# The first load of six rows goes over two DMA queues instead of one

## The chip, the cores and the metric

The kernel runs on one core of one Trainium2 chip. Its time is the device time in microseconds of one execution, and the figure for a kernel is the median of its runs. Beside the timed runs, one execution was taken by the hardware profiler. All durations in the text come from that execution.

## The reference

There are 16 x 1024 = 16,384 tokens with a hidden size of 512, and eight experts. For each token the router's logits are turned into probabilities, the two largest are kept and normalized, and the token's row of x is written out twice, each copy multiplied by one of the two weights:

```
probs        = softmax(router_logits)                    # (16, 1024, 8)
topk_indices = argsort(probs)[..., -2:]
topk_probs   = probs at topk_indices, divided by their sum
out          = x[:, :, None, :].repeat(2, axis=2) * topk_probs[..., None]
```

The output (16, 1024, 2, 512) is twice as large as x. All is float32. The two normalized weights of a token depend only on the difference of its two largest logits.

## The kernel before, in words

**Tiling.** 128 partitions hold 128 tokens of each row index. A token's 512 values are 2 KB, so a "row" of the kernel is 128 tokens, 2 KB on each partition. There are 128 rows in two groups, `GROUPS = [65, 63]`. Within a group each partition holds consecutive tokens, so a load of n rows is, for each of the 128 partitions, one contiguous run of n x 2 KB in HBM.

**Buffers.** `xs` holds the x rows of a group (65 rows of 512 values on each partition). `osp` holds 18 output rows (each 2 x 512). Output rows are written either to `osp` or into parts of `xs` whose input rows have been used up. `WA` holds the two weights of all rows. The logits and the scratch space for finding the two largest lie in `osp`, too, before any output does.

**Order.** The loads of the first group are of 6, 28 and 31 rows, those of the second of 16, 16 and 31 (`LOADS`). Right after the load of six rows come the two loads of the logits, L125 and L126. All of these loads are issued by SyncE (SP), in program order, so they go through one DMA queue in that order. `top2_weights` (L26 to L38) follows: VectorE finds the two largest by maxima and minima, L36 takes the difference into `dlt`, and ScalarE (ACT) makes the two weights with two sigmoids (L37, L38), ahead of which stands the load of its function table.

**The multiplies and stores.** For each piece of `STORES`, VectorE multiplies the x rows by the weights (L133), and a DMA stores the piece (L145). The first piece has three rows, and its store is issued by ACT on its own DMA queue; all other stores are issued by SP. The loads of the second group wait until the stores out of `xs` have freed their places.

SP's queue is called q1 in the profile and ACT's q10. "SPq" and "ACTq" are the instructions on those engines that issue DMAs.

Of the kernel before, what the change touches and what calls it, by code (L numbers as in the profile page):

```python
# [1 line left out]

# [4 lines left out]

F32 = mybir.dt.float32
ALU = mybir.AluOpType
ACTF = mybir.ActivationFunctionType  # L10
P = 128


def top2_weights(nc, WA, dlt, room, logits, E):

    tt = nc.vector.tensor_tensor
    hi, lo, n = None, None, E  # L20
    while n > 1:
        n //= 2
        if hi is None:
            a, b = logits[:, :, 0:n], logits[:, :, n : 2 * n]
            nhi, nlo = room(n), b
            tt(nhi, a, b, op=ALU.max)  # L26
            tt(nlo, a, b, op=ALU.min)  # L27
        else:
            a, b = hi[:, :, 0:n], hi[:, :, n : 2 * n]
            nhi, nlo, tmp = room(n), room(n), room(n)  # L30
            tt(tmp, lo[:, :, 0:n], lo[:, :, n : 2 * n], op=ALU.max)  # L31
            tt(nlo, a, b, op=ALU.min)  # L32
            tt(nlo, nlo, tmp, op=ALU.max)  # L33
            tt(nhi, a, b, op=ALU.max)  # L34
        hi, lo = nhi, nlo
    tt(dlt, hi[:, :, 0], lo[:, :, 0], op=ALU.subtract)  # L36
    nc.scalar.activation(WA[:, :, 0], dlt, ACTF.Sigmoid, scale=-1.0)  # L37
    nc.scalar.activation(WA[:, :, 1], dlt, ACTF.Sigmoid, scale=1.0)  # L38

GROUPS = [65, 63]

LOADS = [[6, 28, 31], [16, 16, 31]]
BASE = [0, 1]

STORES = [
    [(0, 3, "osp", 0), (3, 15, "osp", 3), (18, 16, "xs", 0), (34, 15, "osp", 0), (49, 16, "xs", 33)],
    [(0, 16, "osp", 2), (16, 16, "xs", 0), (32, 15, "osp", 0), (47, 16, "xs", 32)],
]  # L50

L = 18

FREE = [3, 2]


@with_exitstack
def kernel(
    ctx: ExitStack,
    tc: tile.TileContext,  # L60
    x: bass.AP,
    router_logits: bass.AP,
    k: bass.AP,
    out: bass.AP,
):
    nc = tc.nc
    B, S, D = x.shape
    E = router_logits.shape[-1]
    N = B * S
    assert int(k) == 2 and E == 8 and N == P * sum(GROUPS)  # L70
    M = N // P

    x_v, o_v, rl_v = [], [], []
    t0 = 0
    for n in GROUPS:
        t1 = t0 + P * n
        x_v.append(
            x.rearrange("b s d -> (b s) d")[t0:t1].rearrange("(p m) d -> p m d", p=P)
        )
        o_v.append(  # L80
            out.rearrange("b s k d -> (b s) k d")[t0:t1].rearrange(
                "(p m) k d -> p m k d", p=P
            )
        )
        rl_v.append(
            router_logits.rearrange("b s e -> (b s) e")[t0:t1].rearrange(
                "(p m) e -> p m e", p=P
            )
        )
        t0 = t1  # L90

    wpool = ctx.enter_context(tc.tile_pool(name="wpool", bufs=1))
    xs = wpool.tile([P, max(GROUPS), D], F32)
    osp = wpool.tile([P, L, 2, D], F32)
    WA = wpool.tile([P, M, 2], F32)
    dlt = wpool.tile([P, M], F32)


    flat = osp.rearrange("p l k d -> p (l k d)")
    taken = [0]  # L100

    def room(n):
        o = taken[0]
        taken[0] += M * n
        return flat[:, o : o + M * n].rearrange("p (m n) -> p m n", n=n)

    logits = room(E)

    def place(where, at, n):

        if where == "osp":
            return osp[:, at : at + n]
        return xs[:, at : at + 2 * n, :].rearrange("p (r k) d -> p r k d", k=2)

    m0 = 0
    for g, G in enumerate(GROUPS):
        x0, r = BASE[g], 0
        for n in LOADS[g]:
            tc.keep_in_program_order(
                nc.sync.dma_start(xs[:, x0 + r : x0 + r + n, :], x_v[g][:, r : r + n, :])  # L120
            )
            r += n
            if g == 0 and r == 6:
                n0 = GROUPS[0]
                tc.keep_in_program_order(nc.sync.dma_start(logits[:, :n0], rl_v[0]))  # L125
                tc.keep_in_program_order(nc.sync.dma_start(logits[:, n0:], rl_v[1]))  # L126
                top2_weights(nc, WA, dlt, room, logits, E)
        assert r == G
        for r, n, where, at in STORES[g]:
            og = place(where, at, n)  # L130
            again = where == "osp" and at == 0 and r > 0
            for a, b in [(0, FREE[g]), (FREE[g], n)] if again else [(0, n)]:
                nc.vector.tensor_tensor(  # L133
                    og[:, a:b],
                    xs[:, x0 + r + a : x0 + r + b, :]
                    .unsqueeze(2)
                    .to_broadcast([P, b - a, 2, D]),
                    WA[:, m0 + r + a : m0 + r + b, :]
                    .unsqueeze(3)
                    .to_broadcast([P, b - a, 2, D]),  # L140
                    op=ALU.mult,
                )

            queue = nc.scalar if g == r == 0 else nc.sync
            tc.keep_in_program_order(queue.dma_start(o_v[g][:, r : r + n], og))  # L145
        m0 += G


# [1 line left out]
_INS = ['x', 'router_logits', 'k']  # L150
_OUTS = [((16, 1024, 2, 512), 'float32')]

_NUMBERS = {'k': 2}


# [26 lines left out]
```

## Time and profile before

| | |
|---|---|
| median of 3 runs | 240.02 us (239.95 to 240.07) |
| the profiled execution | 239.92 us |
| its span | 238.1 us |
| VectorE busy | 141.9 us (60%) |
| ScalarE busy | 1.8 us |
| read from HBM, written to it | 34.08 MB, 67.11 MB |
| DMA over the span | 425 GB/s on average, 2448 packets |
| queue q1 (SP), q10 (ACT) | 99.62 MB, 1.57 MB |

The span runs from the first to the last recorded instruction of the execution; the profiled execution's own time is 1.8 us longer. The page's DMA row gives the mean busy share of the core's 16 DMA engines in forty slices of the span. A DMA is split into packets, each of which one of the 16 DMA engines carries out. In this kernel a packet is one partition's contiguous run, so a load or store on 128 partitions has 128 packets, and each engine gets eight. A small completion packet per engine follows. The record of a packet has its queue, start, size and duration; it does not name the engine.

A group in a view of busy time by stages counts a packet's bytes and time in the stretch where the packet starts, so a share can be above 1 in a short stretch and below it in the next.

### The profile page before, as it was taken

What the parts mean: (1) busy time and instruction counts of PE and PEld (TensorE: products, weight loads), DVE (VectorE), ACT (ScalarE), POOL (GpSimd) and SP (SyncE); (2) the same over time, 40 slices, a digit from 0 to 9 for tenths busy, and PEclk for the clock granted to TensorE, in tenths of its full rate; (3) what the DMA queues carried; (4) which work ended last, traced back from release to release, by engine and by line L of the source; (5) the groups of instructions that cost most, each with busy time, mean ns of one, the idle gap of its engine ahead of it and who ended that gap; (6) DMA issues with size and microseconds to landing.
All of it is one profiled execution on the core that took longest, in us unless ns stands there. A gap on an engine that the chain in (4) does not pass through costs nothing.

```text
span 238.1 us, 102 instructions
## 1 busy us (share of the span) xinstructions
DVE 141.9 (60%) x22; ACT 1.8 (1%) x3; POOL 0.2 (0%) x4
## 2 busy tenths in 40 slices
DVE  0650499999699999100000699999406999950000
ACT  2000000000000000000000000000000000000000
POOL 0000000000000000000000000000000000000000
DMA  7979998979999999989899999898989999989894
GB/s 265 550 337 500 430 418 374 506 330 495 429 429 407 473 423 402 495 352 528 352 440 435 435 446 501 352 495 374 506 374 462 418 407 451 475 351 517 352 528 176
DMA packets 2448, 101.19 MB, mean 425 GB/s; under 512 B 272, under 2 KB 400, under 8 KB 528
## 3 DMA queue, kind: packets, MB, share of 16 engines
q1 hardware_dynamic: 2304, 99.62, 97.2%
q10 hardware_dynamic: 144, 1.57, 1.5%
HBM read 34.08 MB, written 67.11 MB: 425 GB/s over the span
## 4 chain that ended last, share of the span: by engine, by line
DMA 48%; DVE 40%; SPq 1%; issue 0%; DVEq 0%
DMA xs<-in_x_dram 26%; DVE osp L133 25%; DMA out_dram<-osp 22%; DVE xs L133 14%; SPq L125 0%; SPq L126 0%; SPq L120 0%; SPq L145 0%; DVEq L133 0%
## 5 line engine op out<-in xcount | busy, mean ns | idle before, releaser
L133 DVE TENSOR_TENSOR osp<-xs,WA 128x3072 f32<-128x3072 f32 (+5 forms) x7 | 69.4, 9908 | 61.6 <-DMA xs<-in_x_dram 47.5
L133 DVE TENSOR_TENSOR xs<-xs,WA 128x16384 f32<-128x16384 f32 x4 | 68.9, 17224 | 0.1
L26 DVE TENSOR_TENSOR osp<-osp 128x512 f32<-128x512 f32 x1 | 0.7, 692 | 8.1 <-DMA osp<-in_router_logits_dram 8.1
L37 ACT ACT_TABLE_LOAD x1 | 1.3, 1283 | 0.7 <-PEq L163 0.7
L27 DVE TENSOR_TENSOR osp<-osp 128x512 f32<-128x512 f32 x1 | 0.7, 691 | 0.0
L34 DVE TENSOR_TENSOR osp<-osp 128x256 f32<-128x256 f32 (+1 forms) x2 | 0.7, 352 | 0.0
L32 DVE TENSOR_TENSOR osp<-osp 128x256 f32<-128x256 f32 (+1 forms) x2 | 0.7, 352 | 0.0
L31 DVE TENSOR_TENSOR osp<-osp 128x256 f32<-128x256 f32 (+1 forms) x2 | 0.7, 352 | 0.0
L33 DVE TENSOR_TENSOR osp<-osp 128x256 f32<-128x256 f32 (+1 forms) x2 | 0.7, 351 | 0.0
L37 ACT ACTIVATE WA<-dlt 128x128 f32<-128x128 f32 x1 | 0.3, 314 | 10.1 <-DVE dlt L36 10.1
L36 DVE TENSOR_TENSOR dlt<-osp 128x128 f32<-128x128 f32 x1 | 0.3, 291 | 0.0
L38 ACT ACTIVATE WA<-dlt 128x128 f32<-128x128 f32 x1 | 0.3, 298 | 0.0
L163 POOL MEMSET const-bfloat16-1.0<- 128x1 bf16 x1 | 0.1, 101 | 0.0
L163 POOL MEMSET const-uint8-127<- 128x1 uint8 x1 | 0.1, 101 | 0.0
L163 POOL MEMSET const-float32-0.0<- 128x1 f32 x1 | 0.1, 98 | 0.2 <-issue 0.2
L163 POOL MEMSET const-float32-1.0<- 128x1 f32 x1 | 0.1, 98 | 0.0
## 6 DMA issues: line engine op xcount, KB each, us to landing
out_dram<-osp SPq DMA_DIRECT2D x3, 7680.0 KB, 23.4
xs<-in_x_dram SPq DMA_DIRECT2D x2, 7936.0 KB, 41.7
xs<-in_x_dram SPq DMA_DIRECT2D x2, 4096.0 KB, 40.4
xs<-in_x_dram SPq DMA_DIRECT2D x1, 7168.0 KB, 24.8
xs<-in_x_dram SPq DMA_DIRECT2D x1, 1536.0 KB, 6.0
out_dram<-osp ACTq DMA_DIRECT2D x1, 1536.0 KB, 24.8
osp<-in_router_logits_dram SPq DMA_DIRECT2D x1, 260.0 KB, 6.2
osp<-in_router_logits_dram SPq DMA_DIRECT2D x1, 252.0 KB, 6.4
```

The lines of the kernel that those rows point to most:

```text
L26: tt(nhi, a, b, op=ALU.max)
L27: tt(nlo, a, b, op=ALU.min)
L31: tt(tmp, lo[:, :, 0:n], lo[:, :, n : 2 * n], op=ALU.max)
L32: tt(nlo, a, b, op=ALU.min)
L33: tt(nlo, nlo, tmp, op=ALU.max)
L34: tt(nhi, a, b, op=ALU.max)
L36: tt(dlt, hi[:, :, 0], lo[:, :, 0], op=ALU.subtract)
L37: nc.scalar.activation(WA[:, :, 0], dlt, ACTF.Sigmoid, scale=-1.0)
L38: nc.scalar.activation(WA[:, :, 1], dlt, ACTF.Sigmoid, scale=1.0)
L133: nc.vector.tensor_tensor(og[:, a:b], xs[:, x0 + r + a : x0 + r + b, :] .unsqueeze(2) .to_broadcast([P, b - a, 2, D]), WA[:, m0 + r + a : ...
L163: nc = _bacc.Bacc("TRN2", target_bir_lowering=False, num_devices=1)
```

## The change

The first load of the first group, six rows, is split by partitions. SP loads partitions 0 to 63 and ACT loads partitions 64 to 127 of the same six rows. All other loads stay as they were, on SP with all 128 partitions.

```diff
         for n in LOADS[g]:
-            tc.keep_in_program_order(
-                nc.sync.dma_start(xs[:, x0 + r : x0 + r + n, :], x_v[g][:, r : r + n, :])
-            )
+
+            halves = [(nc.sync, 0, P // 2), (nc.scalar, P // 2, P)]
+            for queue, p0, p1 in halves if g == r == 0 else [(nc.sync, 0, P)]:
+                tc.keep_in_program_order(
+                    queue.dma_start(
+                        xs[p0:p1, x0 + r : x0 + r + n, :], x_v[g][p0:p1, r : r + n, :]
+                    )
+                )
             r += n
```

On SP the first instruction that issues a DMA now covers 64 partitions x 3,072 values instead of 128 x 3,072; the number and order of its instructions stay. On ACT one new DMA (64 x 3,072) stands first, ahead of the load of the function table, the two sigmoids and the store. VectorE's list of instructions is the same.

## The prediction

> **What bounds the kernel now.** I read the page's busy table and its slices first, then busy time by stages, then the timeline and the waits of the start, then the records of single DMA packets.
>
> ```profile
> DVE 141.9 (60%) x22; ACT 1.8 (1%) x3; POOL 0.2 (0%) x4
> DMA  7979998979999999989899999898989999989894
> DMA packets 2448, 101.19 MB, mean 425 GB/s; under 512 B 272, under 2 KB 400, under 8 KB 528
> ```
>
> No compute engine is busy all the time: VectorE has 60%. The DMA row is full in nearly every slice. Busy time by stages (columns: stretch, length, DVE, ACT, POOL, clock, DMA share, GB/s) says the same with less noise:
>
> ```profile
> 0.00:1.70 1.70, 0.00 (x0) 0.98 (x1) 0.20 (x4) 1.00 0.00 0
> 1.70:6.40 4.70, 0.00 (x0) 0.30 (x1) 0.00 (x0) 1.00 0.98 364
> 6.40:20.00 13.60, 7.18 (x12) 0.51 (x2) 0.00 (x0) 1.00 1.02 433
> 45.00:236.90 191.90, 116.68 (x9) 0.00 (x0) 0.00 (x0) 1.00 0.99 429
> 236.90:238.10 1.20, 0.00 (x0) 0.00 (x0) 0.00 (x0) 1.00 0.00 0
> ```
>
> From 1.7 us to 236.9 us the sixteen DMA engines work without a pause. The first load (1.70 to 6.40) is the one stage below the usual rate, 364 against 429 to 433 GB/s. The packet records show why: each engine takes eight packets of 12,288 B, one per partition, in sixteen-wide waves. The first wave starts at 1.73 to 2.35 us and its packets take 949 ns on average; those of the seven waves after it take 460 to 495 ns on average. So the opening latency costs about 0.5 us, once. Later packets are paced almost exactly: 2,116 ns for 57,344 B (27.1 GB/s per engine), 2,418 ns for 65,536 B, loads and stores alike.
>
> What matters for any edit: **does a queue ever run dry?** The stores are issued well before their first packet: at 43.09 us (first packet at 47.15), 79.01 (84.58), 194.61 (198.83), 211.87 (216.95). The smallest lead is 4.1 us. So the end is the start of the stream plus the engine time of all packets. A microsecond more of engine time anywhere is a microsecond at the end; moving VectorE's work by less than 4 us alone is worth nothing.
>
> The start, from the timeline:
>
> ```profile
> 0.72 1.28 ACT L37 ACT_TABLE_LOAD   x1 [0.72 <-PEq L163]
> 0.72 0.37 SPq L120 DMA_DIRECT2D xs<-in_x_dram  x1
> 1.15 0.43 SPq L125 DMA_DIRECT2D osp<-in_router_logits_dram  x1
> 1.62 0.42 SPq L126 DMA_DIRECT2D osp<-in_router_logits_dram  x1
> 2.09 0.99 SPq L120 DMA_DIRECT2D xs<-in_x_dram  x2
> 8.14 0.69 DVE L26 TENSOR_TENSOR osp<-osp 128x512 f32<-128x512 f32 x1 [8.14 <-DMA osp<-in_router_logits_dram]
> 12.06 0.31 ACT L37 ACTIVATE WA<-dlt 128x128 f32<-128x128 f32 x1 [10.06 <-DVE dlt L36]
> 12.61 3.36 DVE L133 TENSOR_TENSOR osp<-xs,WA 128x3072 f32<-128x3072 f32 x1 [0.58 <-ACT WA L38]
> 16.00 0.37 ACTq L145 DMA_DIRECT2D out_dram<-osp  x1
> ```
>
> **The change, part by part.** *Issue.* SP's first DMA stays first but covers 64 partitions; ACT gets one new DMA, about 0.37 us (its later one at 16.00 took that), put ahead of its table load. Both engines are released at 0.72 us, so both halves are issued side by side. Behind ACT's issue are the 1.28 us table load, then done near 2.4 instead of 2.0 us, and the sigmoid, which waits for dlt until 12.06: 0 us, covered by some 9.6 us. On SP the two logits loads and the 28- and 31-row loads are queued behind the first issue. Should 64 descriptors take half of its 0.37 us, SP would be 0.2 us early, and only the opening packets could gain. One more completion packet per engine, 9 ns each in the records: 0.01 us.
>
> *Waits.* The first multiply (12.61) now needs two completions, and sits behind the logits and the sigmoids as before. The logits packets follow SP's half in its ring and take turns with the tail of ACT's half. They land when both the x bytes and the logits are through, as now. Nothing on VectorE moves unless the stream does.
>
> *Engine time of the halves.* This is the only term that can be large. Per half it is four packets of 12,288 B per engine instead of eight (if all sixteen engines serve a half), and the bytes are the same. The trace has no transfer on fewer than 128 partitions. So I bound it:
>
> - Lowest: the packets keep 460 ns, 8 x 460 ns = 3.68 us per engine as now, 0 us added. Below that, the opening wave could shrink: 0.62 us between its first and last start, half of it gone if each queue's descriptors are made in parallel, -0.31 us, and at best the 0.5 us of latency behind the other half's packets: -0.81 us in all.
> - Two queues taking turns: the first store, 1.57 MB on ACT's queue between the loads, has packets of 460 ns, and two of the load waves around it took 2,296 and 2,507 ns instead of 2,116. That is 0.18 + 0.39 = 0.57 us for the same number of bytes.
> - Highest: a transfer's rate goes with the partitions it reaches. Then sixteen engines that write 64 partitions have two engines for one lane, 920 ns a packet, and the eight packets take 7.36 us: +3.68 us.
>
> Which end? The row it is nearest to is the engines' pace. It is the same 27 GB/s for reads from HBM and for writes to it, and each engine has the same share of the partitions, eight, in every transfer. That is how a fixed lane per eight partitions would look. The alternative, that the pace is the engine's own, looks the same in this trace. I take the lane as likelier, because nothing on the HBM side (load or store, 12 or 64 KB) changes the pace.
>
> With lanes shared by two, the sum is not the full 3.68 us, for the engines alternate between the two halves and are out of step. If one is d ahead of its partner, it writes alone for d, shares 2 x (460 - d), and a packet costs 920 - d. So the loss is 460 - d for each of eight packets. In the third wave the sixteen starts lie between 3.11 and 3.56 us; partners eight places apart in that order are about 0.45 x 8/15 = 0.24 us apart, and the loss is 8 x (0.46 - 0.24) = 1.8 us. Neighbours would be 0.03 us apart: 3.4 us. The pair most in step sets the end, since no engine's later queue has slack. With individual starts off the even spacing by up to 0.08 us, the worst pair has d = 0.16 us: 8 x 0.30 = **+2.4 us**. That is my value, an estimate from these rows.
>
> [...]
>
> *Sum.* The profiled run took 239.92 us (span 238.1 and 1.8 around it), 0.10 under the median of 240.02. 239.92 + 2.4 + 0.01 = 242.3 for such a run, 242.4 for the median. The likeliest case's own range is 241.4 (d near 0.3) to 243.4 (neighbours in step).
>
> **The rivals.**
> 1. *Only the queue changes* (0.20). The pace is the engine's own, and a half costs half. For it: sixteen engines at an unchanged 27 GB/s everywhere. Against: nothing here writes 64 partitions. 0 to +0.57 us: 240.0 to 240.6, mostly within 0.2%.
> 2. *The opening gets shorter* (0.08), the other side. Two queues fill the sixteen rings in parallel and hide the slow first wave. It decides if the halves keep 460 ns and the stagger of 0.62 us comes from one issuer. -0.5 to -0.8 us: 239.2 to 239.5. Against: an engine can't use more than its pace, and only 0.81 us is idle there at all.
> 3. *In step* (0.20). Both halves start together on every engine, all sixteen write the same 64 partitions, then the others. +3.7 us: 243.7. For it: the same order in every ring. Against: the 0.45 us spread that the waves keep.
> 4. *The change isn't what it says*: a half might be served by eight engines only. If both halves get the same eight, the price is that of rival 3; with separate eights it is that of rival 1. It is counted in those.
>
> **How the numbers follow.** Two-way sharing out of step has 0.52, rivals 1 to 3 have 0.20, 0.08 and 0.20. About 0.2% (0.48 us) is what a measurement of this kernel can tell from no change. Slower by more than that: 0.52 + 0.20 + a quarter of rival 1 = 0.77. Within it: the rest of rival 1 and a little of rival 2, 0.16. Faster: 0.07. The range runs from 239.9, which takes in rival 1, to 244.0, rival 3 with some of the 0.57 us of taking turns on top. Left out are rival 2 and the tail above, about 0.12.
>
> **What would show each step.** If I am right: first packets still near 1.7 us, both queues alternating on every engine, packets of 12,288 B that take 600 to 900 ns instead of 460; the first load landed near 9 us instead of 6.7, VectorE's first instruction near 10.5 instead of 8.14, the store on ACT's queue at 18.4 instead of 16.0, and every later start late by the same 2.4 us, with the 57,344 B packets back at 2,116 ns. If the packets keep 460 ns, the lane was wrong and rivals 1 or 2 hold. Packets near 920 ns throughout mean rival 3. A first load that is late while the end isn't would mean that the stream has slack I did not see. A table load or a sigmoid that VectorE waits for would show my cover on ACT wrong.

## The result and the profile after

The changed kernel takes 243.18 us (median; 242.95 to 243.28), the kernel before 240.00 us (239.95 to 240.07). The ratio is 1.0129, with a 95% interval of 1.0118 to 1.0141: slower by 3.2 us. The profiled execution took 243.22 us with a span of 241.4 us, 3.3 us more than before's 238.1.

The page's busy rows of the changed kernel:

```profile
DVE 141.9 (59%) x22; ACT 1.8 (1%) x3; POOL 0.2 (0%) x4
DMA packets 2464, 101.19 MB, mean 419 GB/s; under 512 B 288, under 2 KB 416, under 8 KB 544
```

VectorE's busy time and the bytes are unchanged. The sixteen additional packets are the completions of the new DMA, one per DMA engine. Together with the busy share of 0.99 in the next view (sixteen packets in flight at nearly all times) this says that the half loads use all sixteen engines, four packets each; rival 4, a half on eight engines only, is not seen. The records don't name the engine, so this is a reading of the counts. What changed is the rate. Busy time by stages of the changed kernel (stretch, length, DVE, ACT, POOL, clock, DMA share, GB/s):

```profile
1.70:9.10 7.40, 0.00 (x0) 0.90 (x1) 0.00 (x0) 1.00 0.99 217
48.50:240.10 191.60, 116.56 (x9) 0.00 (x0) 0.00 (x0) 1.00 0.99 428
240.10:241.40 1.30, 0.00 (x0) 0.00 (x0) 0.00 (x0) 1.00 0.00 0
```

In the opening stretch the DMA engines are busy (share 0.99) but move 217 GB/s, where before they moved 364 in 1.70 to 6.40. The rest of the stream is as it was, 428 against 429 GB/s, only later. Here a busy share near 1 goes with 217 GB/s as well as with 428: the share does not show the rate, GB/s does.

The start of the changed kernel, from its timeline:

```profile
0.72 0.54 SPq L123 DMA_DIRECT2D xs<-in_x_dram  x1
0.73 0.55 ACTq L123 DMA_DIRECT2D xs<-in_x_dram  x1
1.32 1.28 ACT L37 ACT_TABLE_LOAD   x1 [1.32 <-PEq L168]
1.32 0.56 SPq L130 DMA_DIRECT2D osp<-in_router_logits_dram  x1
12.06 0.69 DVE L26 TENSOR_TENSOR osp<-osp 128x512 f32<-128x512 f32 x1 [12.06 <-DMA osp<-in_router_logits_dram]
15.98 0.32 ACT L37 ACTIVATE WA<-dlt 128x128 f32<-128x128 f32 x1 [13.38 <-DVE dlt L36]
16.53 3.36 DVE L138 TENSOR_TENSOR osp<-xs,WA 128x3072 f32<-128x3072 f32 x1 [0.58 <-ACT WA L38]
19.92 0.35 ACTq L150 DMA_DIRECT2D out_dram<-osp  x1
```

VectorE starts at 12.06 us instead of 8.14, and the first store is issued at 19.92 instead of 16.00, both 3.9 us late. The table load is pushed to 1.32 us, and no one waits for it. The page's DMA issues (KB each, us from issue to landing), the first row from the kernel before, the others from the changed one:

```profile
xs<-in_x_dram SPq DMA_DIRECT2D x1, 1536.0 KB, 6.0
xs<-in_x_dram SPq DMA_DIRECT2D x1, 768.0 KB, 6.4
xs<-in_x_dram ACTq DMA_DIRECT2D x1, 768.0 KB, 10.2
osp<-in_router_logits_dram SPq DMA_DIRECT2D x1, 260.0 KB, 10.0
```

Half of the bytes on SP's queue take longer (6.4 us) than all of them did (6.0 us), and ACT's half lands another 3.8 us later.

The packet records complete the account. The 128 packets of 12,288 B of the first load take 889 ns on average instead of 529: 8 x 0.36 = +2.9 us per engine. The stream's first packet starts at 2.05 instead of 1.73 us: +0.3. The logits' packets, some of them beside the tail of ACT's half, take 124 ns instead of 84: 16 x 0.04 = +0.6. Then 0.5 to 0.6 us are given back: the 57,344 B packets around the first store, of which two waves were slow before (2,296 and 2,507 ns), take 2,116 to 2,160 ns in all waves. The sum is 2.9 + 0.3 + 0.6 - 0.57 = 3.2 us, against 3.3 us by the spans.

### The profile page after: what moved, and what is told of

The parts are those of the page before. It is cut to its first block, busy times and chain, and to the rows that moved or that the text cites. A ratio compares the mean times of both kernels' runs of the same rounds, so it can differ in the third digit from the quotient of the medians.

```text
span 241.4 us, 105 instructions
## 1 busy us (share of the span) xinstructions
DVE 141.9 (59%) x22; ACT 1.8 (1%) x3; POOL 0.2 (0%) x4
## 4 chain that ended last, share of the span: by engine, by line
DMA 49%; DVE 39%; SPq 1%; issue 0%; DVEq 0%
DMA xs<-in_x_dram 26%; DVE osp L138 25%; DMA out_dram<-osp 22%; DVE xs L138 14%; SPq L130 0%; SPq L123 0%; SPq L131 0%; SPq L150 0%; DVEq L138 0%
```

## The experiments

**Halves on one queue, and two queues without halves.** The change does two things at once: it splits by partitions, and it uses a second queue. The first two runs do one each. (The code changes shown in this section are shortened: they give queue, partitions and rows, not the full lines. A minus sign marks the line of the changed kernel or, in the part on what was given back, of the kernel before.)

```diff
-halves = [(nc.sync, 0, P // 2), (nc.scalar, P // 2, P)]
+halves = [(nc.sync, 0, 64), (nc.sync, 64, P)]
```

> Both halves of the first load are issued by SP, one after the other; nothing new on ACT's queue. Theory A (the lane: sixteen engines that write 64 partitions share eight lanes, two to a lane): the 12,288 B packets take about 900 ns as in the changed kernel, the stream is 2.7 to 3.3 us longer, 242.7 to 243.4 us. Theory B (the cost comes from two queues taking turns on the same engines): packets 460 ns, 240.0 to 240.3 us.

Measured: 242.89 us (242.79 to 243.26), ratio 1.0128 (1.0114 to 1.0142). That is the changed kernel's price without its second queue. The packets take 896 ns on average. The opening stretch of this kernel:

```profile
2.00:8.80 6.80, 0.00 (x0) 0.01 (x1) 0.00 (x0) 1.00 1.06 231
```

Its start, where the two halves are merged in the first row:

```profile
0.72 1.18 SPq L124 DMA_DIRECT2D xs<-in_x_dram  x2
0.72 1.28 ACT L37 ACT_TABLE_LOAD   x1 [0.72 <-PEq L170]
```

Two halves need 1.18 us to issue while no other engine issues a DMA, 0.59 us each against 0.37 us for one whole load. So the longer issue goes with the halves too.

The other part alone, with SP on rows 0 to 2 and ACT on rows 3 to 5:

```diff
-halves = [(nc.sync, 0, P // 2), (nc.scalar, P // 2, P)]
+halves = [(nc.sync, rows 0:3, all partitions), (nc.scalar, rows 3:6, all partitions)]
```

> Two queues without halves of the partitions: SP loads rows 0 to 2 and ACT rows 3 to 5 of the first load, each on all 128 partitions (6,144 B packets, sixteen per engine in all). Theory A (lane): packets at their usual pace, about 230 ns, and only the slower opening of two issues side by side, +0.3 us: 240.0 to 240.5 us. Theory B (two queues): about +3 us, 243 us.

Measured: 240.04 us beside 239.97 of the kernel before, ratio 1.0008 (0.9999 to 1.0017). The same bytes over the same two queues cost nothing that can be told from no change, and gain nothing. This kernel's opening stretch and issues:

```profile
1.70:6.50 4.80, 0.00 (x0) 0.74 (x1) 0.00 (x0) 1.00 0.97 361
xs<-in_x_dram SPq DMA_DIRECT2D x1, 768.0 KB, 5.9
xs<-in_x_dram ACTq DMA_DIRECT2D x1, 768.0 KB, 6.1
```

361 GB/s, and both pieces land within 6.1 us. Even the +0.3 us that I allowed for two issues side by side was wrong: each took 0.38 to 0.40 us. Theory B, two queues taking turns, falls.

**Does the cost grow with the bytes?** The 28-row load was split in the first one's place.

> The first load is whole, on SP, as before; the second load (28 rows, packets of 57,344 B) is split in two halves of the partitions over SP and ACT in its place. Theory A (lane): the cost grows with the bytes, the packets take nearly twice their 2.116 us, 8 x 1.7 to 2.1 us = +13.6 to +16.9 us: 253.6 to 257 us. Theory D (a fixed cost per packet or per half, as a slow opening would be): at most the changed kernel's +3.2 us again, 243.2 us or less.

Measured: 259.68 us, ratio 1.0825 (1.0810 to 1.0839): 19.7 us slower, above the range of theory A, and theory D falls. The 128 packets of 57,344 B take 4,327 ns (SP) and 4,302 ns (ACT) on average, where those of the kernel before take 2,189 with the slow ones around the store: they alone make 17.0 us more of each engine's time. ACT's half was issued after the first sigmoid, at 12.58 us, and its first packet started at 20.07. So SP's half ran alone for a while, and was just as slow. This kernel's stages:

```profile
7.20:20.00 12.80, 7.18 (x12) 0.51 (x2) 0.00 (x0) 1.00 1.03 220
20.00:37.30 17.30, 0.00 (x0) 0.00 (x0) 0.00 (x0) 1.00 1.00 212
```

220 GB/s with nothing but partitions 0 to 63 in flight once the last logits are through (7.6 us): no second transfer is needed for the price. The packet records account for the remaining 2.7 us, too: all packets together take 19.6 us more of each engine than before, with no pause in the stream. Of this, 0.9 us is in the 63,488 B packets beside ACT's half, of which 32 take 2,788 instead of 2,342 ns. Another 1.4 us is in two waves far behind the halves, each the last one ahead of a change between loads and stores: stores of 65,536 B at 138.0 us with 3,167 instead of 2,418 ns, and loads of 63,488 B at 176.8 us with 3,022 ns, where the kernel before has 2,423. Why these two are slow stays open.

**Which 64 partitions?** If the price is that of too few partitions, any 64 pay it. If partitions 0 to 63 share one limit, and 64 to 127 another (in the run above their packets take 4,327 and 4,302 ns), then partitions 32 to 95, half in each, don't. The expectations call each limit a set of eight lanes; eight times the 27.1 GB/s of one engine is 217 GB/s, as much as the changed kernel's opening moves. I tried it first on the six rows.

```diff
-halves = [(nc.sync, 0, P // 2), (nc.scalar, P // 2, P)]
+pieces = [(nc.sync, 32, 96), (nc.scalar, 0, 32), (nc.scalar, 96, P)]
```

> The first load in three pieces: SP partitions 32 to 95, ACT partitions 0 to 31 and then 96 to 127. Theory A (lane, with partitions 0 to 63 on one set of eight lanes and 64 to 127 on the other): SP's 64 partitions reach all lanes, so its packets take about 460 to 500 ns; ACT's quarters reach eight lanes each and take about 900 ns. About half of the added time, 241.3 to 242.2 us. Theory C (any transfer on fewer than 128 partitions is slow, wherever it lies): SP's packets take about 900 ns as well, 243 us or more.

Measured: 241.91 us, ratio 1.0084 (1.0070 to 1.0097). The time lies where theory A had it, but SP's packets took 829 ns on average and not 460 to 500. The pieces were in flight together, and by theory A they share their lanes, so the run does not tell the theories apart. The next one does, because SP's piece is alone at first:

> The first load is whole. The 28-row load (57,344 B packets) goes as partitions 32 to 95 over SP, and as 0 to 31 and 96 to 127 over ACT, whose pieces are issued after the first sigmoid, so SP's piece runs alone at first. Theory A (lanes; partitions 0 to 63 share eight, 64 to 127 the other eight): SP's 64 partitions reach all lanes, its packets take about 2,116 ns; ACT's 32-partition pieces reach eight lanes and take about 4,300 ns. 4 x 4.3 us instead of 4 x 2.1 us on half of the packets, about +8.6 us: 247.5 to 250 us. Theory C (every transfer on fewer than 128 partitions is slow): SP's packets take 4,300 ns from the first on, and the time is that of the halves or more, 259 us.

All 64 packets of SP's piece took exactly 2,116 ns, the pace of a whole load. ACT's, on 32 partitions each, took 4,188 ns on average. This kernel's stages, SP's piece alone in the first row, ACT's piece on partitions 0 to 31 alone in the second, and a stretch without any DMA in the third:

```profile
7.10:15.60 8.50, 6.72 (x12) 0.51 (x2) 0.00 (x0) 1.00 1.03 447
15.60:23.80 8.20, 0.46 (x1) 0.00 (x0) 0.00 (x0) 1.00 1.04 224
57.00:61.20 4.20, 4.20 (x2) 0.00 (x0) 0.00 (x0) 1.00 0.00 0
12.57 31.67 DMA xs<-in_x_dram
60.55 0.35 SPq L152 DMA_DIRECT2D out_dram<-osp  x1
```

64 partitions load at full rate from 32 to 95 (447 GB/s) and at half rate from 0 to 63 (220), and 0 to 31 are as fast as 0 to 63 (224 against 220 GB/s). Theory C falls: the rate goes with which partitions a transfer reaches, as theory A has it. The runs show these rates; a lane itself is in no record. One thing the runs do not separate: in x the place in HBM changes along with the partition. The logits, which lie elsewhere, are slower in halves too (125 instead of 84 ns a packet, below), so it is likely the partition, but no run moved the one without the other.

The total was missed badly (258.37 us, ratio 1.0757, 1.0731 to 1.0784, instead of at most 250), and the last three rows show why. With the 28 rows landed only at 44.2 us (the fourth row, from the chain that ended last), the store behind VectorE's 15-row multiply is issued only at 60.55 us, and the queues have run dry: 4.6 us without any DMA up to 61.4 us, and another 2.1 us up to 81.8. All idle time of the engines in this run adds up to 7.2 us, next to 11.1 us of added engine time. Of the latter, 8.3 us is in ACT's packets, as expected, and most of the rest in the 63,488 B packets beside them and in the same two later waves as in the run ahead. That the stream never runs dry, as in the kernel before with its smallest lead of 4.1 us, does not hold in this run.

**What was given back.** The slow load packets around the first store are 0.57 us in the kernel before and nearly 0 after. First I delayed the stream by the same amount without halves:

```diff
+if first load: nc.sync.dma_start(osp rows 12 to 14, the same six rows, all partitions)
```

> The kernel before with 1.57 MB more to load: the first six rows are loaded a second time, into a place of osp that is not yet used, on all 128 partitions, behind the first load and ahead of the logits. 128 more packets of 460 ns are 3.68 us of every engine, close to what the halves added (3.72 us by the start of the 28-row load). The question is the 0.57 us that load packets around the first store take too long in the kernel before, and do not in the changed kernel. Theory F (the delay itself moves the store away from what slowed it): the 57,344 B packets take 2,116 ns throughout, 243.0 to 243.3 us. Theory G (it goes only with halves, whose engines leave them in another step): two of the waves are slow again, 243.6 to 243.9 us.

Measured: 243.65 us, ratio 1.0150 (1.0123 to 1.0177). The slow waves are there (2,243 and 2,567 ns). So the delay does not remove them. Next, the first store left the second queue:

```diff
-queue = nc.scalar if g == r == 0 else nc.sync
+queue = nc.sync
```

> The kernel before with its first store issued by SP, so that it follows the loads in one queue instead of taking turns with them on a second one. Its slots in osp are needed again at 60 us, by when it has landed. If the slow load packets (0.57 us) come from the two queues taking turns, they go: 239.3 to 239.6 us. If they come from something else, or come back where the store now stands: 239.9 to 240.2 us.

Measured: 240.35 us beside 240.03, ratio 1.0011 (0.9999 to 1.0022), a little above both ranges. The 57,344 B packets are at 2,116 ns now, but the last wave of the 31-row load, just ahead of the store, takes 3,567 ns instead of 2,400 in the kernel before: the loss moved with the store and grew to 1.2 us. Here it goes with the first change from loads to stores and does not need two queues taking turns. Last, two smaller doses of halves:

```diff
+nc.scalar.dma_start(osp[64:128, 17, 0, 0:16], x_v[0][64:128, 0, 0:16])   # first on ACT's queue
```

> The kernel before and one more DMA, first on ACT's queue: 64 partitions (64 to 127) of 64 B each, into a place of osp that is not yet used. It moves 4 KB, so by the lane its own cost is nil; the longer issue of a 64-partition DMA is on ACT, where nothing waits for it. It asks what removed the 0.57 us of slow load packets in the kernels with halves. Theory H (that a 64-partition DMA was issued at all): the 57,344 B packets take 2,116 ns throughout, 239.3 to 239.6 us. Theory G (that halves with real work leave two engines per lane in step): slow packets as before, 239.9 to 240.2 us.

```diff
-nc.sync.dma_start(logits[:, :n0], rl_v[0]); nc.sync.dma_start(logits[:, n0:], rl_v[1])
+each of the two as partitions 0:64 and 64:128, four DMAs on nc.sync
```

> The first load is whole, on SP; the two loads of the logits are split into halves of the partitions, four DMAs on SP (2,080 B and 2,016 B packets). Theory A (lane): sixteen packets per engine take about 170 instead of 84 ns, +1.3 us. Theory G (halves leave the engines in step, and the slow packets go): -0.57 us on top, 240.5 to 241.0 us. Without that: 241.2 to 241.6 us.

The tiny half: 239.96 us beside 239.92, ratio 1.0003 (0.9994 to 1.0012), with slow waves of 2,197 and 2,513 ns. The logits in halves: 240.21 us, ratio 1.0011 (1.0002 to 1.0020), below every range that I had given. Their packets take 125 ns instead of 84, not the 170 of theory A, and the first wave behind them 2,564 ns: 1.1 us in all. Around the store the waves average 2,116 to 2,120 ns again. So in these runs the loss is gone after a halved load of some size, and not after a DMA that merely has its form. How it does so stays open; that it leaves two engines in step is a guess which no run tested by itself. No version here beat the kernel before.

## Why the prediction was right, and where its steps were off

The forecast was 242.4 us, in a range of 239.9 to 244.0, slower at 0.77. The measured 243.18 us lies within that. It is also within the likeliest case's own range (241.4 to 243.4). That a half loads at half the rate (220 against 433 GB/s once the first load is through), the sign and the missing slack were right. The order of the halves in that likeliest case was not: the engines took one half after the other, as rival 3 has it, and rival 3's 243.7 us is nearer to the result than 242.4.

- *The bound.* The stream of the DMA engines sets the end, without slack: held. The 28-row load's first packets start at 10.89 us instead of 7.17, 3.7 us later, and the span grows by that less what was given back.
- *The mechanism.* That the rate goes with the partitions is shown by the halves on one queue (231 GB/s), by the half that ran alone (220), and by 32 to 95 at full rate (447); that it goes with the partition and not with the place in HBM is argued, as said above. The lane was my picture for the rate. One for every eight neighbouring partitions, which is how the prediction can be read, would have made 32 to 95 slow as well. Rival 1 (only the queue changes) is what the split by rows shows (ratio 1.0008), and it would have been right for that edit. Rival 2 (a shorter opening) had the wrong sign.
- *The size of the lane term.* I took 460 - d per packet, with d = 0.16 us for engines that alternate between the halves: +2.4 us. The measured term is +2.9 us. In the records ACT's first packet starts only at 5.14 us, when all but two of SP's 64 have started: the engines did not alternate but worked through one half and then the other. SP's third and fourth waves take 926 and 958 ns and ACT's four 841 to 936; the six average 910, near rival 3's 920: the offset d is worth some 0.01 us, not 0.16. SP's first two waves lose only 0.03 and 0.18 us (983 and 674 ns, before 949 and 495), in the slow opening, which neither sum had counted. So the term lay between the forecast and rival 3 (+3.7), and the step that was mis-sized is the offset.
- *The issue.* I expected a 64-partition DMA to be issued as fast as before or in half of the time. In the changed kernel it takes 0.54 and 0.55 us instead of 0.37, and the stream starts 0.3 us later. I had that at 0, or a gain.
- *The logits.* That they land "as now" was off: +0.6 us of engine time, some of it beside ACT's tail, a term that the sum lacked.
- *The give-back.* I used the 0.57 us around the first store as the price of two queues taking turns. The runs show that it is neither that nor fixed: two queues cost nothing for the rows (ratio 1.0008), the loss stays with the store (1.2 us where SP issues it), and it is gone behind halves of the six rows (2,116 to 2,160 ns) and of the logits (2,116 to 2,120 ns), not behind a half of 4 KB (2,197 and 2,513 ns). It hid about as much as the logits added: that the sum came nearer than its terms was luck.
- *VectorE's start* was to be at 10.5 us and the store at 18.4. They were at 12.06 and 19.92. The lane term's missing 0.5 us, the issue's 0.3 and the logits' 0.6 make 1.4 of the 1.5 us between them; the give-back comes only later. The first load, forecast to land near 9 us, landed at 10.9 with ACT's half.

## What to carry to other kernels

In this case a load's rate depends on which partitions it reaches (220 GB/s for 0 to 63, 447 for 32 to 95), not only on its bytes; stores in halves were not tried. Where a transfer is to be shared by two queues, split it along the free dimension and keep all 128 partitions (here 240.04 us beside 239.97, where halves took 243.18), and expect nothing from the second queue where the DMA engines are busy anyway, as they were here (share 0.97). In a profile, read GB/s beside the busy share: in the changed kernel's opening the engines look fully busy at half the rate of later (share 0.99 at 217 GB/s, and at 428).

## What the runs showed that I had not expected

- In these runs a DMA on 64 partitions took longer to issue than one on 128. On ACT, side by side with a load on SP, it took 0.54 us for 4 KB on 64 partitions (the tiny half, first row) against 0.40 us for 768 KB on all 128 (the split by rows, second row). The same goes for SP (0.54 against 0.37). Fewer partitions were not always slower: the two DMAs on 32 partitions took 0.37 and 0.44 us (28 rows in three pieces, last rows). And a load of the logits on all 128 partitions right behind a half took 0.56 instead of 0.43 us. The reason stays open.

```profile
0.73 0.54 ACTq L121 DMA_DIRECT2D osp<-in_x_dram  x1
0.73 0.40 ACTq L124 DMA_DIRECT2D xs<-in_x_dram  x1
12.16 0.37 ACTq L124 DMA_DIRECT2D xs<-in_x_dram  x1
12.57 0.44 ACTq L124 DMA_DIRECT2D xs<-in_x_dram  x1
```

- Partitions 32 to 95 loaded at full pace (2,116 ns per 57,344 B packet), partitions 0 to 63 at half (4,327 ns).
- The first change from loads to stores cost 0.57 us when the store came over a second queue and 1.2 us when it followed the loads on one, and close to nothing after a load of the six rows in halves (2,116 to 2,160 ns a packet in all waves). This is no fixed price either: with the 28 rows split, two later changes cost 0.7 to 1.0 us each, where the kernel before pays less than 0.1.
